# Two-stream feed-forward blocks: gate and up products by seven block products, inner dimension in three chunks

## The chip, the cores and the metric

One NeuronCore of a Trainium2 chip runs the kernel. The metric is the device time of one execution in microseconds (us); shorter is better. The engines are PE (matrix products), DVE (elementwise work on vectors), ACT (casts and activation functions), POOL (idle here) and SP (which issues the DMA loads). Each works through its own queue in order.

## The reference, cut to what matters

Two stacks of two layers are computed one after the other in float32. The first works on one stream of 256 tokens of width 1024. The second works on two streams, `xs` (256 tokens) and `cs` (256 context tokens), with a modulation vector per stream. The block that the change touches is

```python
def ffn_half_step(s, m, i, norm_g, w_in, w_out):
    h = modulate(rmsnorm(s, norm_g), m, i)
    gu = h @ w_in                       # 1024 -> 2 x 2816
    y = (jax.nn.silu(gu[..., :D_FF]) * gu[..., D_FF:]) @ w_out   # 2816 -> 1024
    return s + 0.5 * gate(m, i) * y

def modulation(cond, w_mod, b_mod):
    m = jax.nn.silu(cond) @ w_mod + b_mod    # 1024 -> 9 x 1024
```

Each layer of the second stack runs `ffn_half_step` (step 0) on both streams, a mixer (step 1) with attention over both, and `ffn_half_step` (step 2). In the last layer, step 2 runs on `xs` alone. So three such blocks run on both streams: (layer 0, step 0), (0, 2) and (1, 0).

## The kernel before, in words

Float32 products are made of three matmuls. `parts` splits a tile into a rounded high part (a cast on ACT) and the rest (a subtraction on DVE, the low part); `mm3` adds high x high, high x low and low x high in PSUM. Weights arrive by DMA in tiles `raw` (four in a ring), and `weights` splits them into `whi` and `wlo` (rings of four each). An instruction that needs a slot of a ring waits until the slot's last reader is done. In `mm3` the low part of the weights is read first by the third matmul of a group.

`ffn2` has 22 pairs of 128 gate columns and 128 up columns. A pair is two products of 8 k-tiles on 512 columns (both streams side by side), then silu and product on ACT and DVE, and a split into `g`. After 11 pairs (a half) come eight down steps `d`, each over the 11 `g`s, and `gated_add` puts them onto the stream. The first pairs of a block are computed on the un-normalised stream (`ahead`, `firsts`) while the norm's factor R is being made (`norm_end`), and are corrected afterwards (`rooted`); these are the cover for the norm and for the building of `h` (`streams`).

The modulation vectors are not matmuls: `mod_step` takes one 128x1024 instruction on DVE per column group and stream (tile `junk`; 256 in all), with its weights in `wm` (two slots, one load of 512 KB for two instructions). They are strewn between the other work, in a fixed order; `mod_in(l, step)` and `mod_out` flush what a step still needs. `mix2` is the mixer: latents, convolution and Fourier parts, then heads (`hd`), with output products over the first four tiles (`wa`) between them and the last four at the end (`wo`).

The order of each engine's queue is what a scheduler made of the program at build time; it is fixed when the kernel runs.

Of the kernel before, what the change touches and what calls it, by code (L numbers as in the profile page):

```python
# [25 lines left out]
NU = {(0, 2): 2, (1, 0): 2, (1, 2): 3}  # L26
# [45 lines left out]
def host_arrays(inp):  # L72
# [28 lines left out]
    o["w2u1"], o["w2d1"] = ups(f["ffn1_w_in_2"]), downs(f["ffn1_w_out_2"])  # L101
    o["w2u2"], o["w2d2"] = ups(f["ffn2_w_in_2"]), downs(f["ffn2_w_out_2"])
# [109 lines left out]
class Net:  # L212
# [41 lines left out]
    def r4(self, *shape, more=False):  # L254
        if more:
            x = self.t("r4b", [P, 1028], 4, F32R, pool=self.p_second)
        else:
            x = self.t("r4", [P, 1028], 15, F32R)
# [228 lines left out]
    def mod_out(self, l, step):  # L487
# [3 lines left out]
        for s in range(2):  # L491
# [6 lines left out]
            self.G[s] = G  # L498

# [441 lines left out]
    def ffn1(self, l, R):  # L941
# [4 lines left out]
        first = self.first_two(pre, (0,))  # L946
# [34 lines left out]
        for d in range(KD):  # L981
            if l == 1 and d == 5:

                self.mod_in(0, 0)
                self.h_c = [self.r4(2, 512, more=k >= 4) for k in range(KD)]
            ps = self.ps()[:, :T]
            for half in range(2):
                for k0, k1 in ((0, 6), (6, 11)):
# [3 lines left out]
                    if l == 1 and d in (5, 6):  # L992
                        k = 4 * (d - 5) + 2 * half + (k0 > 0)
                        with self.tc.issue_after(self.split.ins):
                            self.h2(1, self.Rc, self.h_c[k], k)
# [5 lines left out]
            self.add_x(st, d, ps)  # L1001
            if d == 5:
                self.warm(st["sq"])
# [23 lines left out]
    def ahead(self, s, d, n4):  # L1027

        nc = self.nc
        if d == 0 and s == 0:  # L1030
            self.pre2 = []
        if s == 0:

            x = self.r4(1028, more=d >= n4)
            self.pre2.append([[x[:, o:o + n] for o in (b, b + n)] for b, n in ((0, T + 2), (516, T))])
# [37 lines left out]
    def first_two(self, h, order):  # L1073

        W = self.first
        pss = [self.ps() for _ in W]
        for s in order:
            c = slice(s * T, s * T + T)
            for k in range(KD):
                for w, ps in zip(W, pss):  # L1080
                    self.mm3(ps[:, c], (w[0][:, k, :], w[1][:, k, :]), [x[:, c] for x in h[k]], k == 0, k == KD - 1)
        return [ps[:, :len(order) * T] for ps in pss]
# [6 lines left out]
    def ffn2(self, l, step, Rs, nh, ng, n4):  # L1089
        nc, a = self.nc, self.a  # L1090
        ns = len(Rs)
        N = ns * T
        wu, wd = ("w2u1", "w2d1") if step == 0 else ("w2u2", "w2d2")
        third = a[wu][l, 2]
        if l == 0 and step == 0:

            order, xs = (1, 0), self.h_c
            W = self.streams(Rs, (0,), xs, third)
            nu = 1
        else:  # L1100
            order = None
            nu = NU[(l, step)]
            first = self.firsts(ns, [a[wu][l, i] for i in range(2, 2 * nu)])
            third = a[wu][l, 2 * nu]
            xs = [self.r4(2, 512, more=k >= nh) for k in range(KD)]
            W = self.streams(Rs, range(ns), xs, third)
        h = [(x[:, 0, :N], x[:, 1, :N]) for x in xs]
        X = (self.xs, self.cs)
        out = [{} for _ in range(ns)]
        Rs_in, Rs = Rs, []  # L1110
        final = self.next is None
        rate = 2 if l == 0 and step == 0 else 1
        for half in range(2):
            g = []
            for jj in range(HF):
                j = half * HF + jj
                if j >= nu:
                    pss = []
                    for i in range(2):
                        pss.append(self.times(W if 2 * j + i == 2 * nu else a[wu][l, 2 * j + i], h, N))  # L1120
                        self.mod_step(rate)
                elif order:
                    pss = self.first_two(h, order)
                s = self.f2()[:, :N]
                if j >= nu or order:
                    nc.scalar.activation(s, pss[0], AF.Silu)
                    nc.vector.tensor_tensor(s, s, pss[1], ALU.mult)  # L1127
                else:
                    s2 = self.f2()[:, :N]
                    bs = self.rooted((s, s2), first[j], Rs_in)  # L1130
                    for i in range(ns):
# [434 lines left out]
```

## Time and profile before

| | |
|---|---|
| median of 3 runs | 2477.66 us (2476.97 to 2477.69) |
| the profiled execution | 2476.86 us |
| its span, first to last instruction | 2475.1 us |
| PE busy | 2456.9 us, 99% |
| weight loads on PE | 2170.2 us, 88% |
| DVE busy | 1812.9 us, 73% |
| ACT busy | 1197.4 us, 48% |
| mean granted TensorE clock | 0.999 of full speed |

Busy times are shares of one profiled execution; what an engine does while PE is busy costs nothing by itself. Matmuls are pipelined, so the interval between their starts, not their recorded duration, is what one takes.

### The profile page before, as it was taken

What the parts mean: (1) busy time and instruction counts of PE and PEld (TensorE: products, weight loads), DVE (VectorE), ACT (ScalarE), POOL (GpSimd) and SP (SyncE); (2) the same over time, 40 slices, a digit from 0 to 9 for tenths busy, and PEclk for the clock granted to TensorE, in tenths of its full rate; (3) what the DMA queues carried; (4) which work ended last, traced back from release to release, by engine and by line L of the source; (5) the groups of instructions that cost most, each with busy time, mean ns of one, the idle gap of its engine ahead of it and who ended that gap; (6) DMA issues with size and microseconds to landing.
All of it is one profiled execution on the core that took longest, in us unless ns stands there. A gap on an engine that the chain in (4) does not pass through costs nothing.

```text
span 2475.1 us, 39396 instructions
## 1 busy us (share of the span) xinstructions
PE 2456.9 (99%) x15211; PEld 2170.2 (88%) x15211; DVE 1812.9 (73%) x3180; ACT 1197.4 (48%) x2084; POOL 1.2 (0%) x14
## 2 busy tenths in 40 slices
PE   8999999999999999999999999999999999999998
PEld 7999999899999988888887888888888888898998
DVE  8888887988998886776757875655765643688654
ACT  7766665856665522223536632223532223567544
POOL 0000000000000000000000000000000000000000
PEclk9999999999999999999999999999999999999999
DMA  7555657545666664654311344544345742234563
GB/s 251 172 156 181 199 183 235 183 152 172 216 215 205 202 197 149 211 182 125 115 59 42 120 147 127 177 145 125 123 147 163 244 153 74 91 117 139 178 206 120
DMA packets 123851, 395.91 MB, mean 160 GB/s; under 512 B 14352, under 2 KB 17168, under 8 KB 123408
## 3 DMA queue, kind: packets, MB, share of 16 engines
q1 hardware_dynamic: 123664, 393.41, 51.1%
q8 instruction: 119, 1.95, 0.3%
q14 instruction: 68, 0.56, 0.1%
HBM read 392.30 MB, written 1.05 MB: 159 GB/s over the span
## 4 chain that ended last, share of the span: by engine, by line
PE 95%; DVE 2%; ACT 1%; DMA 0%; issue 0%; SPq 0%; DVEq 0%; ACTq 0%
PE wops L305 13%; PE wops L303 13%; PE wops L304 13%; PE dnps L304 6%; PE dnps L305 6%; PE dnps L303 6%; PE upps L305 3%; PE upps L303 3%; PE upps L304 3%; PE qkvps L304 1%; PE qkvps L305 1%; PE qkvps L303 1%; PE cvps L303 1%; PE cvps L305 1%; PE cvps L304 1%; PE latps L304 1%
## 5 line engine op out<-in xcount | busy, mean ns | idle before, releaser
L298 ACT CAST wowhi<-woraw 128x1024 fp32r<-128x1024 f32 (+3 forms) x266 | 246.4, 928 | 581.9 <-PE wops L304 359.6
L305 PE MATMUL wops<-wor,wowlo 128*128 128x512 f32 (+2 forms) x1371 | 480.5, 351 | 0.0
L303 PE MATMUL wops<-wor,wowhi 128*128 128x512 f32 (+2 forms) x1371 | 478.9, 350 | 0.0
L304 PE MATMUL wops<-wor,wowhi 128*128 128x512 f32 (+2 forms) x1371 | 478.6, 349 | 0.0
L299 DVE TENSOR_TENSOR wowlo<-woraw,wowhi 128x1024 fp32r<-128x1024 f32 (+3 forms) x266 | 283.9, 1071 | 216.9 <-ACT wowhi L298 208.7
L304 PEld LDWEIGHTS wops<-wor,wowhi 128*128 128x128 f32 x1371 | 258.0, 188 | 38.0 <-DVE wor L1042 0.2
L305 PEld LDWEIGHTS wops<-wor,wowlo 128*128 128x128 f32 x1371 | 257.9, 188 | 36.5
L303 PEld LDWEIGHTS wops<-wor,wowhi 128*128 128x128 f32 x1371 | 257.5, 188 | 36.5
L298 ACT CAST dnwhi<-dnraw 128x768 fp32r<-128x768 f32 (+2 forms) x144 | 125.1, 871 | 290.7 <-PE dnps L304 184.6
L299 DVE TENSOR_TENSOR dnwlo<-dnraw,dnwhi 128x768 fp32r<-128x768 f32 (+2 forms) x144 | 143.8, 1000 | 69.5 <-ACT dnwhi L298 66.9
L305 PE MATMUL upps<-hr,upwlo 128*128 128x256 f32 x656 | 183.2, 280 | 1.5 <-DVE upwlo L299 1.5
L304 PE MATMUL upps<-hr,upwhi 128*128 128x256 f32 x656 | 183.9, 281 | 0.0
L303 PE MATMUL upps<-hr,upwhi 128*128 128x256 f32 x656 | 183.8, 280 | 0.0
L468 DVE SCALAR_TENSOR_TENSOR dnjunk<-dnwm,cond 128x1024 bf16<-128x1024 f32 x134 | 163.5, 1220 | 2.9 <-DMA dnwm<-in_wm 1.7
L305 PE MATMUL dnps<-dnr,dnwlo 128*128 128x512 f32 (+1 forms) x371 | 142.4, 384 | 0.0
L304 PE MATMUL dnps<-dnr,dnwhi 128*128 128x512 f32 (+1 forms) x371 | 142.2, 383 | 0.0
L303 PE MATMUL dnps<-dnr,dnwhi 128*128 128x512 f32 (+1 forms) x371 | 142.1, 383 | 0.0
L468 DVE SCALAR_TENSOR_TENSOR wojunk<-wowm,cond 128x1024 bf16<-128x1024 f32 x114 | 138.9, 1219 | 0.0
L305 PEld LDWEIGHTS upps<-hr,upwlo 128*128 128x128 f32 x656 | 123.2, 188 | 2.3 <-DVE upwlo L299 2.3
L303 PEld LDWEIGHTS upps<-hr,upwhi 128*128 128x128 f32 x656 | 123.6, 188 | 0.0
L304 PEld LDWEIGHTS upps<-hr,upwhi 128*128 128x128 f32 x656 | 123.1, 188 | 0.0
L1127 DVE TENSOR_TENSOR wof<-wof,wops 128x512 f32<-128x512 f32 (+1 forms) x59 | 35.5, 602 | 110.2 <-PE wops L305 110.2
(690 smaller groups left out, 6197.9 us busy)
## 6 DMA issues: line engine op xcount, KB each, us to landing
woraw<-in_w2u SPq DMA_DIRECT2D x132, 512.0 KB, 3.7
upraw<-in_w1u SPq DMA_DIRECT2D x82, 512.0 KB, 4.3
wowm<-in_wm SPq DMA_DIRECT2D x73, 512.0 KB, 4.4
dnwm<-in_wm SPq DMA_DIRECT2D x67, 512.0 KB, 4.2
dnraw<-in_w2u SPq DMA_DIRECT2D x44, 512.0 KB, 4.2
woraw<-in_w2d SPq DMA_DIRECT2D x48, 384.0 KB, 3.1
woraw<-in_w2d SPq DMA_DIRECT2D x48, 320.0 KB, 2.9
qkvraw<-in_w1q SPq DMA_DIRECT2D x24, 512.0 KB, 4.4
```

The lines of the kernel that those rows point to most:

```text
L298: act = self.nc.scalar.copy(hi, src)
L299: return act, self.nc.vector.tensor_tensor(lo, src, hi, ALU.subtract)
L303: mm(ps, L[0], R[0], start=st, stop=False)
L304: mm(ps, L[0], R[1], start=False, stop=False)
L305: mm(ps, L[1], R[0], start=False, stop=sp)
L468: nc.vector.scalar_tensor_tensor(junk, self.wm, 1.0, self.cond[:, s, :], ALU.mult, ALU.mult, accum_out=self.M[l][s][step][:, j:j + 1])
L1127: nc.vector.tensor_tensor(s, s, pss[1], ALU.mult)
```

## The change

A new `ffn2s` replaces `ffn2` for the three two-stream blocks; `ffn2` remains for the last, single-stream one. Two pairs are made un-normalised as before. The other 20 are a 2x2 block product: rows are the streams, columns gate and up, and the inner 1024 is cut in halves. By Strassen's scheme (Winograd's form) it takes seven block products of 4 k-tiles on 256 columns in place of two products of 8 k-tiles on 512. `sums` builds the seven moving operands (x1, x2, c2, t1 to t4) once per block; `seven` builds, per pair, the seven stationary ones from four 128x512 sums on DVE and four splits: A (11 and 12), B (s2 and s1), C (s3 and 22), D (s4 alone). `begin`, `middle` and `ends` issue the products and what joins them; the last two products of a pair are issued within the next pair. The inner 22 of the down product is cut in chunks of 8, 7 and 7 instead of two halves of 11, so there are 24 down steps a block, each with one weight tile, in place of 16 with two.

The modulation work is spread anew: one `junk` in a pair (all of chunks 1 and 2, the last two of chunk 0), one or two in a down step, and for (0, 2) also in the mixer's projections, its `wa` phase, and a flush `mod_in(l, 2)` in its `wo` phase. Some buffers move: `r4b` has 8 tiles in place of 4, K, Q and the rope table use it, and `es` has two of 1024 in place of three of 512. Block (0, 0) now also makes its first pairs un-normalised.

```diff
-NU = {(0, 2): 2, (1, 0): 2, (1, 2): 3}
+NU = 2
+CHUNKS = ((0, 8), (8, 15), (15, 22))
...
+    def seven(self, gate, up):
+
+        nc = self.nc
+        r1, r2 = self.raw(gate), self.raw(up)
+        h = slice(0, 4), slice(4, 8)
+        s = self.t("es", [P, 1024], 2, pool=self.p_second).rearrange("p (a b) -> p a b", a=8)
+        W = {}
+
+        def split(x, a, b=None):
+            n = x.shape[1]
+            hi, lo = [self.t(t, [P, 1024], 4, F32R)[:, :n * P].rearrange("p (a b) -> p a b", a=n)
+                      for t in ("whi", "wlo")]
+            self.split = self.parts(hi, lo, x)[1]
+            W[a] = hi[:, h[0]], lo[:, h[0]]
+            if b:
+                W[b] = hi[:, h[1]], lo[:, h[1]]
+
+        add = lambda o, a, b: nc.vector.tensor_tensor(o, a, b, ALU.add)
+        split(r1, "11", "12")
+        add(s[:, h[1]], r2[:, h[0]], r2[:, h[1]])
+        add(s[:, h[0]], s[:, h[1]], r1[:, h[0]])
+        split(s, "s2", "s1")
+        add(r2[:, h[0]], r2[:, h[0]], r1[:, h[0]])
+        split(r2, "s3", "22")
+        add(r1[:, h[1]], s[:, h[0]], r1[:, h[1]])
+        split(r1[:, h[1]], "s4")
+        return W
+
+    def product(self, ps, W, B, st, sp):
+        for k in range(4):
+            self.mm3(ps, (W[0][:, k, :], W[1][:, k, :]), self.B7[B][k], st and k == 0, sp and k == 3, True)
...
+                u = self.begin(a[wu][l, 2 * j], a[wu][l, 2 * j + 1])
+                if n or jj >= 6:
+                    self.mod_step(1)
+                if todo:
+                    todo.pop(0)()
+                self.middle(u, todo.pop(0) if todo else lambda: None)
+                x = self.r4(2, 512, more=gmore(jj))
+                g.append((x[:, 0], x[:, 1]))
+                todo = self.ends(u, g[-1])
+            for f in todo:
+                f()
+            if n == 2:
+                self.mod_in(*((l, 1) if step == 0 else (1, 0)))
...
+                self.mod_step(1 if c < 4 else 2, (l, 2, 16))
...
             W = self.weights_half(a["w2o"][l, d, :, 0:4])
+            self.mod_step(1, (l, 2, 16))
```

How the queues change is seen at three places. Names carry the tile's number, and `waits` the engines or DMA queues that must have come so far.

On DVE, one pair of the block (0, 2) before: `wof` is silu(gate) times up, `wor` its low part, `wowlo` low parts of weights, `wojunk` modulation.

```order
L1127 TENSOR_TENSOR wof22887_16241<-wof22887_16241,wops2885_16214 128x512 [waits PE_49,Activation_49]
L299 TENSOR_TENSOR wowlo2910_16359<-woraw2908_16356,wowhi2909_16358 128x1024 [waits DMAHW0_49,Activation_49]
L299 TENSOR_TENSOR wor42888_16244<-wof22887_16241,wor42888_16244 128x512 [waits Activation_49]
L468 SCALAR_TENSOR_TENSOR wojunk2912_16387,M110_139<-wowm2906_16352,cond_471 128x1024
L299 TENSOR_TENSOR wowlo2917_16398<-woraw2915_16395,wowhi2916_16397 128x1024 [waits DMAHW2_49,PE_49,Activation_49]
L468 SCALAR_TENSOR_TENSOR wojunk2920_16428,M100_136<-wowm2919_16426,cond_471 128x1024 [waits DMAHW4_49,DVE_49]
```

A pair had six rows, two of them modulation, and no sum of weights among them.

On DVE, one steady pair in the second chunk of the block (0, 0) now. Low parts: `upwlo2108` is C, `upwlo2110` is D, `upwlo2125` is the next pair's A and `upwlo2127` its B. `upes` and `upraw` with L1161 are sums of weights; L1213, L1218 and L1220 belong to the previous pair's result, `upr4b` is its low part.

```order
L1161 TENSOR_TENSOR upes2123_12696<-upes2123_12696,upraw2121_12692 128x512 [waits DMAHW2_49,DVE_49]
L304 TENSOR_TENSOR upwlo2108_12576<-upraw2101_12561,upwhi2107_12575 128x1024 [waits Activation_49]
L304 TENSOR_TENSOR upwlo2110_12581<-upraw2100_12559,upwhi2109_12580 128x512 [waits PE_49,Activation_49]
L473 SCALAR_TENSOR_TENSOR upjunk2116_12617,M001_131<-upwm2115_12615,cond_471 128x1024 [waits DMAHW7_49]
L1213 SCALAR_TENSOR_TENSOR upf22094_12481<-upps2091_12453,upf22094_12481 128x256
L1161 TENSOR_TENSOR upraw2122_12694<-upraw2122_12694,upraw2121_12692 128x512
L1218 TENSOR_TENSOR upf22094_12481<-upf12096_12511,upsc2097_12530 128x256 [waits PE_49]
L304 TENSOR_TENSOR upwlo2125_12698<-upraw2121_12692,upwhi2124_12697 128x1024 [waits Activation_49]
L1220 SCALAR_TENSOR_TENSOR upf22094_12481<-upf12098_12555,upf22094_12481 128x256 [waits Activation_49]
L1161 TENSOR_TENSOR upraw2121_12692<-upes2123_12696,upraw2121_12692 128x512 [waits DVE_49]
L304 TENSOR_TENSOR upwlo2127_12704<-upes2123_12696,upwhi2126_12703 128x1024 [waits PE_49,Activation_49]
L304 TENSOR_TENSOR upr4b2099_12558<-upf22094_12481,upr4b2099_12558 128x512 [waits Activation_49]
```

The low part of the next A now stands behind D's low part, a junk, a sum of weights and two instructions of the previous pair.

On PE, within the pair whose tiles are 2103 (A), 2105 (B), 2107 (C) and 2109 (D), where the fourth product of the queue ends and the fifth begins:

```order
L308 MATMUL upps2111_12584<-tr41876_11177,upwhi2105_12570 128x256
L309 MATMUL upps2111_12584<-tr41876_11177,upwhi2105_12570 128x256
L310 MATMUL upps2111_12584<-tr41876_11177,upwlo2106_12571 128x256
L308 MATMUL upsc2097_12530<-tr41850_11091,upwhi2089_12449 128x256 [waits DVE_49]
L309 MATMUL upsc2097_12530<-tr41850_11091,upwhi2089_12449 128x256
L310 MATMUL upsc2097_12530<-tr41850_11091,upwlo2090_12450 128x256
```

The fifth product, s4 times c2, is the previous pair's: it reads `upwhi2089`, the previous D, whose slot the present D (`upwhi2109`) takes.

On DVE, the `wo` phase of the layer 0 mixer, before (a gated add is L1086 there, L1042 builds the next block's un-normalised operands, L316 the norm's sum of squares):

```order
L1086 SCALAR_TENSOR_TENSOR xs_75<-wops2745_15435,hdMG2530_14504,xs_75 128x256 [waits PE_49]
L1086 SCALAR_TENSOR_TENSOR cs_8279<-wops2745_15435,hdMG2531_14506,cs_8279 128x256
L299 TENSOR_TENSOR wowlo2772_15568<-woraw2770_15565,wowhi2771_15567 128x512 [waits DMAHW4_49,Activation_49]
L316 TENSOR_TENSOR woS2562739_15417<-woS2562739_15417,wonq2746_15449 128x256 [waits Activation_49]
L1042 SCALAR_TENSOR_TENSOR wor42747_15452<-xs_75,woMA2733_15390,wor42747_15452 128x256 [waits DVE_49,Activation_49]
L316 TENSOR_TENSOR woS2562741_15425<-woS2562741_15425,wonq2748_15458 128x256 [waits Activation_49]
L1042 SCALAR_TENSOR_TENSOR wor42747_15452<-cs_8279,woMA2734_15394,wor42747_15452 128x256 [waits DVE_49,Activation_49]
L1086 SCALAR_TENSOR_TENSOR xs_75<-wops2752_15469,hdMG2530_14504,xs_75 128x256 [waits PE_49]
L1086 SCALAR_TENSOR_TENSOR cs_8279<-wops2752_15469,hdMG2531_14506,cs_8279 128x256
```

And the same phase now, towards its end (a gated add is L1103 here, the norm's sum L321):

```order
L1103 SCALAR_TENSOR_TENSOR cs_8279<-wops2917_16815,hdMG2654_15740,cs_8279 128x256
L473 SCALAR_TENSOR_TENSOR wojunk2879_16678,M002_132<-wowm2878_16676,cond_471 128x1024 [waits DMAHW5_49,DVE_49]
L321 TENSOR_TENSOR woS2562899_16737<-woS2562899_16737,wonq2920_16838 128x256 [waits Activation_49]
L473 SCALAR_TENSOR_TENSOR wojunk2880_16680,M012_135<-wowm2878_16676,cond_471 128x1024 [waits DVE_49]
L1103 SCALAR_TENSOR_TENSOR xs_75<-wops2924_16849,hdMG2653_15738,xs_75 128x256 [waits PE_49]
L473 SCALAR_TENSOR_TENSOR wojunk2882_16684,M002_132<-wowm2881_16682,cond_471 128x1024 [waits DMAHW6_49,DVE_49]
L321 TENSOR_TENSOR woS2562897_16729<-woS2562897_16729,wonq2925_16863 128x256 [waits Activation_49]
L473 SCALAR_TENSOR_TENSOR wojunk2883_16686,M012_135<-wowm2881_16682,cond_471 128x1024 [waits DVE_49]
L304 TENSOR_TENSOR wor4b2926_16866<-woMb2890_16700,wor4b2926_16866 128x2
L1103 SCALAR_TENSOR_TENSOR cs_8279<-wops2924_16849,hdMG2654_15740,cs_8279 128x256
L473 SCALAR_TENSOR_TENSOR wojunk2885_16690,M002_132<-wowm2884_16688,cond_471 128x1024 [waits DMAHW7_49,DVE_49]
```

Between two gated adds now stand four junks or so; the phase has 22 of them, and none before.

## Rows read from the trace of the kernel before

**Rows 1.** The page, first lines: span, then busy time of each engine.

```profile
span 2475.1 us, 39396 instructions
PE 2456.9 (99%) x15211; PEld 2170.2 (88%) x15211; DVE 1812.9 (73%) x3180; ACT 1197.4 (48%) x2084; POOL 1.2 (0%) x14
```

**Rows 2.** PE's waits in the whole span: total us, times, longest.

```profile
PE qkvps L303 <- ACT r L528: 6.3, 1, 6.3
PE upps L305 <- DVE upwlo L299: 1.5, 3, 0.6
...
PE dnps L304 <- DVE dnr4b L1016: 0.2, 1, 0.2
```

**Rows 3.** Windows of 50 us: two-stream FFN, then single-stream FFN.

```profile
core 0: us, PE busy (x) PEld busy (x) DVE busy (x) ACT busy (x) POOL busy (x), PEclk, DMA share, GB/s
1500.00:1550.00 50.00, 50.00 (x217) 40.43 (x216) 28.64 (x46) 11.64 (x16) 0.00 (x0) 1.00 0.43 127
...
2300.00:2350.00 50.00, 50.00 (x425) 50.00 (x424) 30.89 (x43) 23.44 (x38) 0.00 (x0) 1.00 0.58 182
```

**Rows 4.** Timeline of DVE in the l0 step 2 FFN's entry: start, duration, instruction.

```profile
1434.78 0.69 DVE L299 TENSOR_TENSOR wor<-wof,wor 128x512 fp32r<-128x512 f32 x1
1435.39 1.22 DVE L299 TENSOR_TENSOR wowlo<-woraw,wowhi 128x1024 fp32r<-128x1024 f32 x1
1436.52 1.22 DVE L468 SCALAR_TENSOR_TENSOR wojunk<-wowm,cond 128x1024 bf16<-128x1024 f32 x1
1437.66 0.08 DVE L468 DVE_READ_ACCUMULATOR wojunk<-wowm,cond 128x1 f32 x1
```

**Rows 5.** Timeline of PE, then DVE, at the start of that FFN.

```profile
1409.19 0.28 PE L305 MATMUL wops<-hdr4b,wowlo 128*128 128x256 f32 x1
...
1410.72 0.49 DVE L1013 SCALAR_TENSOR_TENSOR wof<-xs,woMA,woR 128x256 f32<-128x256 f32 x1
1411.12 0.48 DVE L1042 SCALAR_TENSOR_TENSOR wor<-cs,woMA,wor 128x256 fp32r<-128x256 f32 x1
...
1413.23 0.42 DVE L340 TENSOR_TENSOR wonq<-wonq,wonq 128x256 f32<-128x256 f32 x1
1413.57 0.48 DVE L1013 SCALAR_TENSOR_TENSOR wof<-xs,woMA,woR 128x256 f32<-128x256 f32 x1
1413.96 0.41 DVE L341 SCALAR_TENSOR_TENSOR woR<-wonq,wonq 128x256 f32<-128x256 f32 x1
1414.30 2.35 DVE L299 TENSOR_TENSOR wowlo<-woraw,wowhi 128x1024 fp32r<-128x1024 f32 x2
```

**Rows 6.** One of ACT's groups by form, 1460 to 1770 us: busy us, mean ns.

```profile
L298 ACT CAST wor<-wof 128x512 fp32r<-128x512 f32 x12 | 7.5, 621 | 0.3 <-DVE wof L1127 0.3
```

**Rows 7.** Timelines: PE to ACT to DVE (1818 us), DVE to PE (651 us).

```profile
1818.39 0.39 PE L304 MATMUL wops<-wor,wowhi 128*128 128x512 f32 x1
...
1818.82 1.05 ACT L298 CAST wowhi<-woraw 128x1024 fp32r<-128x1024 f32 x1 [3.91 <-PE wops L304]
...
1819.90 1.23 DVE L299 TENSOR_TENSOR wowlo<-woraw,wowhi 128x1024 fp32r<-128x1024 f32 x1 [2.58 <-ACT wowhi L298]
...
651.07 1.22 DVE L299 TENSOR_TENSOR upwlo<-upraw,upwhi 128x1024 fp32r<-128x1024 f32 x1
...
652.35 0.39 PE L305 MATMUL upps<-hr,upwlo 128*128 128x256 f32 x1 [0.63 <-DVE upwlo L299]
```

**Rows 8.** Windows of 50 us in the heads' phases, l0 mixer, then l1 mixer.

```profile
1250.00:1300.00 50.00, 50.00 (x250) 41.64 (x249) 26.46 (x42) 17.24 (x29) 0.00 (x0) 1.00 0.15 48
...
1350.00:1400.00 50.00, 49.98 (x277) 38.33 (x276) 37.26 (x90) 30.85 (x80) 0.00 (x0) 1.00 0.32 101
...
2200.00:2250.00 50.00, 48.93 (x321) 42.00 (x320) 38.56 (x82) 35.69 (x80) 0.00 (x0) 1.00 0.20 64
```

**Rows 9.** The page, loads: KB each, median us from issue to landing.

```profile
woraw<-in_w2u SPq DMA_DIRECT2D x132, 512.0 KB, 3.7
...
wowm<-in_wm SPq DMA_DIRECT2D x73, 512.0 KB, 4.4
```

More of the change, by code (lines that the diff above doesn't have):

```diff
@@ L984, in ffn1 @@
                 self.mod_in(0, 0)
-                self.h_c = [self.r4(2, 512, more=k >= 4) for k in range(KD)]
+                for k in range(5):
+                    self.ahead(0, k, 0)
             ps = self.ps()[:, :T]
@@ new lines, in ends, with first, second @@
+    def ends(self, u, out):
+        nc = self.nc
+        W, r1, r3, y = u["W"], u["r1"], u["r3"], u["y"]
+        def first():
+            self.product(r1, W["22"], "t4", False, True)
+            nc.vector.scalar_tensor_tensor(y[:, :T], r1, -1.0, y[:, :T], ALU.mult, ALU.mult)
+        def second():
+            self.product(r3, W["s4"], "c2", False, True)
+            c = y[:, T:]
+            nc.vector.tensor_tensor(c, u["u2"], r3, ALU.add)
+            nc.scalar.activation(c, c, AF.Silu)
+            nc.vector.scalar_tensor_tensor(c, u["u3"], -1.0, c, ALU.mult, ALU.mult)
+            self.parts(out[0], out[1], y)
+        return [first, second]
@@ L1090, in ffn2, with ffn2s @@
+    def ffn2s(self, l, step, Rs, tmore, gmore, n4):
         nc, a = self.nc, self.a
-        ns = len(Rs)
-        N = ns * T
         wu, wd = ("w2u1", "w2d1") if step == 0 else ("w2u2", "w2d2")
[L1094 to L1106, printed above, removed]
@@ L1113, in ffn2 @@
+        return Rs
+    def ffn2(self, l, step, R, nh, ng):
+        nc, a = self.nc, self.a
+        wu, wd = "w2u2", "w2d2"
+        nu = 3
+        self.phase = "e"
+        first = self.firsts(1, [a[wu][l, i] for i in range(2, 2 * nu)])
+        xs = [self.r4(2, 512, more=k >= nh) for k in range(KD)]
+        W = self.streams([R], (0,), xs, a[wu][l, 2 * nu])
+        h = [(x[:, 0, :T], x[:, 1, :T]) for x in xs]
+        out = {}
         for half in range(2):
@@ new lines, in ffn2 @@
+                    Ws.append((k0, k1, self.weights(a[wd][l, d, :, half * HF + k0:half * HF + k1, :])))
+                for k0, k1, W in Ws:
+                    for k in range(k0, k1):
+                        self.mm3(ps, (W[0][:, k - k0, :], W[1][:, k - k0, :]), g[k], k == 0, k == HF - 1)
+                if half == 1 and d:
+                    self.turn(d - 1)
+                self.gated_add(0, d, ps)
+                if half == 1:
+                    self.norm_add(out, d, KD, self.xs[:, d, :])
```

280 lines of the change are left out of this document (187 added, 93 removed).

## The prediction

> **What bounds the kernel now.** I read the page first, then PE's waits, then stretches of 50 us, then single rows of the other engines. The page says that PE is busy 99% of the span, DVE 73% [rows 1]. The list of PE's waits confirms it: seven rows, of which the longest is 6.3 us, once, and the other six come to about 4 us in the whole span [rows 2]. So today whatever takes matmul time away shortens the kernel, as long as DVE and ACT keep up, and whatever makes PE wait lengthens it by the wait. The profiled execution took 2476.86 us, 0.8 under the median of the runs (2477.66); the sum is made against it. About 0.2% (5 us) is what a measurement of this kernel can tell from no change.
>
> **What the change takes from PE.** A stretch of pure 512-column matmuls holds 217 in 50 us, 0.2306 us each; one of 256 columns holds 425, 0.1177 us each [rows 3]. A gate/up pair of a two-stream FFN was 2x8x3 = 48 matmuls of 512 columns, 11.07 us. Seven products of 4 k, 3 matmuls each, are 84 of 256 columns, 9.89 us. That is 1.18 us a pair, and 3 FFNs with 20 such pairs are 60: **-70.8 us**, if PE is never kept waiting. Three chunks in place of two halves leave the down products' matmul count alone.
>
> The Trainium skill (TensorE: Matmul & The Clock Gate, section Back-to-back issue gap) speaks against this: it gives about 81 ns for a sustained matmul of 128 columns and about 131 ns for one of 512. Between these an estimate for 256 is 98 ns, and by it the pair would go from 6.3 to 8.2 us of PE, not down. The trace does not agree: here the ratio of the two widths is 0.51 and 512 columns take 0.2306 us.
>
> **What it puts on DVE, pair by pair.** Before, a pair cost DVE two low parts of 128x1024, a 512 product and a 512 low part; consecutive starts give 1.14 us for 1024 (and for a modulation product, "junk"), 0.61 for 512 [rows 4], so 3.5 us, or 5.8 with two junks, of 11.07. Now there are three low parts of 1024 (3.42), four sums of weights, one low part of D and one of g at 512 (6x0.61), two 256 scalar-tensor-tensor (0.40 each) and three 256 tensor-tensor (0.34 each) [rows 5]: 8.9 us, 10.0 with the junk that stands in nearly every pair of chunks 1 and 2. PE needs 9.89. DVE alone would thus be level with PE. But order decides, and it is in-order.
>
> D (the s4 weights) is the fourth tile of a pair in rings of four, so it takes the slot of the previous pair's D. That slot is read until the previous pair's s4 product, and PE has this as the fifth product of the present pair (the order shown). Counting from the pair's first matmul: five products end at 5x1.41 = 7.06. ACT then casts D: 0.04 to start and 0.62 [rows 6, 7], DVE goes 0.03 later: 7.75. Behind it in DVE's row stand D's low part 0.61, junk 1.14, scalar-tensor-tensor 0.40, a sum 0.61, tensor-tensor 0.34: 10.85; and only then the low part of the next pair's A, 1.22 [rows 4], and 0.06 to PE [rows 7]: 12.13. That operand belongs to the third matmul of the next pair, so the next pair begins at 11.9 (12.13 less 2x0.118), not at 9.89. Without the junk it is 10.75. The cycle closes on itself, since the next D again waits for the fifth product. Per chunk the first transition is free (no earlier s4 in the chunk). Chunk 0 has six Strassen pairs and junks in the last two: 3x0.86 + 2.0 = 4.6; chunks 1 and 2 have seven pairs: 5x2.0 each. 24.6 a FFN, **+74 us**. Bounds: 0 (DVE gets to A's low part before D's slot is free, against the order) and 60x2.0 = 120. I take 74, as every link has a row.
>
> **Ends of the chunks.** The last pair's s4 product ends nine products, 12.7 us, after that pair begins. Behind it stand a 256 tensor-tensor, silu, a scalar-tensor-tensor, ACT's cast and the low part of g: 2.9 us with the handovers, and on DVE's row also the low parts of the first down weights (1.14 each) and one junk, three in chunk 2: near 20 where PE, with 6 or 7 k of down work (3x0.2306 us each) in hand, wants it near 17. I take 2.2, 2.3 and 3.9 for the three chunks, 8.4 a FFN, **+25 us**; bounds 0 and 15 a FFN.
>
> **Entries.** PE's last matmul of the stage before runs until 1409.5, the second stream's R is finished at 1414.3 [rows 5]: 4.9 us. The un-normalised pairs give PE 4x8x3x2 matmuls of 256, 22.6 us, as cover; today this is enough, PE does not wait there [rows 2]. After R the row of DVE now has, up to the fourth tile of x1, 4 of 1024, 10 of 512, 23 scalar-tensor-tensor and 12 tensor-tensor: 23.7 us, and up to the second Strassen pair's A 35.5. PE wants this A at 22.6 + 5x1.41 = 29.7 and gets it at about 40. With the stalls so far counted once, 9 to 10 us each, three entries: **+29 us**; bounds 0 and 35.
>
> **Modulation work moved into the mixer.** The l0 mixer's output phase now has the rest of (0, 2) to do at once. On DVE, from its first gated add to the low part of the next FFN's first weights, stand 22 junks (25.1), 32 scalar-tensor-tensor (12.6), 14 tensor-tensor (4.7), 5 of 512 (3.1), 2 of 1024 (2.3) and some small: 48.7 us. PE's eight output steps are 8x12x0.2306 = 22.1. The weights that follow are late by the difference, **+26 us**; bounds 0 (the junks find room earlier) and 37 if wm's two slots set the pace: 11 loads at (4.4 + 2.3)/2 = 3.35 us [rows 9] are 37 us beside 23 of other work, so 60. Before, no junk stood here. In the heads' phases some 19 (l0) and 16 (l1) junks enter; DVE has 11 to 24 us free in 50 there [rows 8], but its work is links of a chain. 35x1.14 = 40 is the upper end, 0 the lower; about a third, **+12 us**, since the row with least room has PE at 48.93 [rows 8].
>
> The down phases (DVE 4.1 to 4.7 us a step of a low part, one or two junks, two gated adds and in chunk 2 the norm, PE 7 or 8 k x 3 x 0.2306 = 4.8 or 5.5) hide their extra 8 steps' gated adds: if the cover went, 24x0.8 = 19 us. Loads: 1 MB of weights a pair and 0.25 of wm. A raw slot frees one pair ahead, some 6.6 us before it is read, against 3.7 to 4.4 us to land [rows 9]: hidden, and if not 1 to 2 us a pair.
>
> **Sum.** 2476.9 - 70.8 + 74 + 25 + 29 + 26 + 12 = **2572 us**, 3.8% slower.
>
> The Trainium skill (Perfetto Trace Analysis, section Optimization Strategy) says that the same gap repeating on the engine that should be saturated can mean too few buffers for the next tile. By this the 2.0 us would recur in every pair of chunks 1 and 2, which is the cycle above; no run here shows it yet.
>
> **Rivals.**
> A. *Faster: the pair is bound by PE.* If DVE reaches A's low part early, since waits in its row end sooner than I count, pairs come every 9.89 us, the cycle's 74 go, and with them most of the tails and of the junk's cost in the heads: -70.8 + 29 + 26 and a few give about 2465; with entries and output phase hidden too, 2406. For it: DVE's work per pair is just at PE's. Against: the slot. It decides where the work between D's slot and A's low part falls by 2.0 us, about one junk and one sum.
> B. *About the same.* Only the cycle holds and junks hide elsewhere: +74 + 0 to 8 cancel the gain: 2477 to 2485. For: wide lower bounds of the other four terms. Against: all four would have to vanish.
> C. *Slower by less.* The cycle is as above and half of 92 for the rest is hidden: 2500 to 2535.
> D. *Loads come late.* Each pair waits 1 us more for raw weights or wm: +60, 2630. Against it: 1.25 MB in 11.9 us is 105 GB/s, and 182 stand in a stretch today [rows 3].
> E. *256-column matmuls with weights of their own cost more than 0.1177.* At 0.132 the gain is nil, and the time 2640. Rows of 256 with as many weight loads as matmuls (425 and 424) speak against it [rows 3].
>
> **Chances.** The forecast with its bounds (2535 to 2625) 0.5, C 0.17, B 0.06 (half of it within 0.2%), A 0.19, D and E 0.08. The range has to reach down to A's 2465 and up to D: 2463 to 2628 leaves out A's lower part and the far end. The likeliest alone has 2535 to 2610. Slower by over 0.2% 0.77, within 0.2% 0.04, faster 0.19.
>
> **What would show it.** In the profile of the changed kernel: about 352 matmuls (84 in 11.9 us) in 50 us of the up stretches of chunks 1 and 2, against 425 for a PE at its peak; in PE's waits a row "<- DVE upwlo" of 2 us, some ten times a FFN, at the third matmul of a pair; waits of 5 to 10 us behind the sums at the three entries; one wait or several, of some 26 us together, at the end of the l0 mixer. DVE near 85 to 100% in the pairs. If the up stretches show 425 and DVE idles, the cycle is wrong and A holds; if PE waits there for ACT after a DMA, it is D; if PE waits for nothing and yet shows under 425, it is E. My weakest terms are the last two: they rest on counted work beside counted cover, not on a row that shows the wait.

## The result and the profile after

| | before | after |
|---|---|---|
| median, same chip | 2477.47 us (4 runs, 2476.97 to 2477.69) | 2495.11 us (4 runs, 2492.55 to 2496.45) |
| ratio | 1 | 1.007 [1.0053, 1.0088] |
| span of the profiled execution | 2475.1 us | 2494.7 us |
| mean granted TensorE clock | 0.999 | 0.985 |

The changed kernel is slower by 0.7%, 17.6 us. The forecast was 2572 us, with 2535 to 2610 called likeliest: the sign came out, the size was wrong by 77 us. The page's first lines, which answer to [rows 1]:

```profile
span 2494.7 us, 44881 instructions
PE 2413.4 (97%) x17383; PEld 2240.9 (90%) x17383; DVE 2165.6 (87%) x3926; ACT 1396.6 (56%) x2494; POOL 1.2 (0%) x14
```

PE is busy 43.5 us less, some of that at a lower clock; DVE is busy 353 us more. PE's waits over the whole span (total, times, longest), the answer to [rows 2]:

```profile
PE upps L308 <- DVE upf L1089: 16.3, 4, 8.4
PE hdtp L1657 <- ACT hdes L1648: 8.9, 5, 4.5
PE wops L310 <- DVE wowlo L304: 8.7, 1, 8.7
PE wops L308 <- DVE cs L1103: 8.5, 2, 5.6
PE upps L310 <- DVE upwlo L304: 6.7, 5, 3.6
PE qkvps L308 <- ACT r L543: 6.0, 1, 6.0
PE hdsc L308 <- ACT hdr4b L303: 4.7, 3, 2.4
PE wotp L330 <- DVE woS L321: 3.5, 1, 3.5
```

Only the `qkvps` row is wholly old. A repeating wait of 2 us at the pairs is not there: `upwlo` is waited for 5 times, not thirty, and three of these (1.5 us) are old ones in the first stack. The new waits lie in few places: the three entries (7.7, 8.9 and 5.9 us, the `upps` rows and some short ones not shown), the l0 mixer's end (`wops`, `wotp`: 20.7) and the heads (`hdtp`, `hdsc` and three short rows not shown: about 17). Windows of the changed kernel, in the form of [rows 3] and [rows 8]:

```profile
core 0: us, PE busy (x) PEld busy (x) DVE busy (x) ACT busy (x) POOL busy (x), PEclk, DMA share, GB/s
850.00:900.00 50.00, 42.36 (x333) 41.37 (x332) 47.12 (x86) 30.65 (x54) 0.00 (x0) 0.90 0.19 66
1100.00:1150.00 50.00, 50.00 (x419) 49.51 (x418) 48.94 (x83) 31.03 (x58) 0.00 (x0) 1.00 0.43 145
1400.00:1450.00 50.00, 32.25 (x202) 29.84 (x203) 46.47 (x105) 22.75 (x47) 0.00 (x0) 0.76 0.43 146
1450.00:1500.00 50.00, 41.13 (x325) 40.76 (x324) 48.43 (x95) 33.38 (x61) 0.00 (x0) 0.90 0.19 64
1800.00:1850.00 50.00, 44.09 (x355) 43.48 (x355) 48.80 (x95) 34.58 (x63) 0.00 (x0) 0.97 0.18 64
2200.00:2250.00 50.00, 40.46 (x213) 32.85 (x214) 38.37 (x74) 24.42 (x50) 0.00 (x0) 0.86 0.56 182
```

The second line is a steady up stretch: 419 matmuls of 256 columns in 50 us, PE busy throughout, DVE at 48.94 of 50. The other lines are entries, the mixer's end and the heads: there PE waits 6 to 18 us and its granted clock falls below 1. Where 0.90 stands, the engine had the lower of its two levels (1.2 of 2.4 GHz) for a fifth of the window.

By stages (boundaries are the first product of the next block in the trace): up to the l0 mixer 11.7 us are won, in (0, 2) 9.4 and in (1, 0) 11.0; the l0 mixer takes 232.4 us in place of 203.2 (+29.2), the l1 mixer 146.5 in place of 126.7 (+19.8), and the last block 2.7 more. The sum is +19.6, the difference of the two spans. Where the 2.7 in the last block come from was not traced.

Why the pair does not wait is seen in one steady pair of chunk 2 in (0, 0), starts and durations on PE, ACT and DVE:

```profile
1119.18 1.05 ACT L303 CAST upwhi<-upraw 128x1024 fp32r<-128x1024 f32 x1 [0.98 <-PE upps L309]
...
1120.27 1.82 DVE L304 TENSOR_TENSOR upwlo<-upraw,upwhi 128x1024 fp32r<-128x1024 f32 x2
1120.56 0.63 ACT L303 CAST upwhi<-upraw 128x512 fp32r<-128x512 f32 x1
...
1121.91 0.28 PE L308 MATMUL upsc<-tr,upwhi 128*128 128x256 f32 x1
...
1123.41 1.06 ACT L303 CAST upwhi<-upraw 128x1024 fp32r<-128x1024 f32 x1 [0.93 <-PE upsc L309]
1124.50 1.23 DVE L304 TENSOR_TENSOR upwlo<-upraw,upwhi 128x1024 fp32r<-128x1024 f32 x1
...
1126.15 0.28 PE L308 MATMUL upps<-tr,upwhi 128*128 128x256 f32 x1
1126.39 0.28 PE L310 MATMUL upps<-tr,upwlo 128*128 128x256 f32 x1
```

The cast of 512 elements is D. It runs at 1120.56, *before* the previous pair's s4 product begins at 1121.91; the forecast let it wait until that product was over. The wait for that product is on the next row, 1123.41, and belongs to the next pair's A. So the ring doesn't go round in order, and the sentence beside the queue order ahead of the prediction, that the present D takes the previous D's slot, is wrong. The trace doesn't name the slots, but the starts fit this: C takes the slot of its own pair's A (free after two products), D that of the previous C, and the next A that of the previous D. The next A's low part ends at 1125.73; PE needs it at 1126.39 and waits for nothing. The period is 9.95 us, from 1116.20 to 1126.15.

### The profile page after: what moved, and what is told of

Same layout as the page of the kernel before. It is cut to its first block, busy times and chain, and to the rows that moved or that the text cites. A ratio compares the mean times of both kernels' runs of the same rounds, so it can differ in the third digit from the quotient of the medians.

```text
span 2494.7 us, 44881 instructions
## 1 busy us (share of the span) xinstructions
PE 2413.4 (97%) x17383; PEld 2240.9 (90%) x17383; DVE 2165.6 (87%) x3926; ACT 1396.6 (56%) x2494; POOL 1.2 (0%) x14
## 4 chain that ended last, share of the span: by engine, by line
PE 85%; DVE 10%; DMA 2%; ACT 2%; issue 1%; SPq 0%; DVEq 0%; ACTq 0%
PE upps L308 9%; PE upps L310 9%; PE upps L309 9%; PE dnps L308 6%; PE dnps L309 6%; PE dnps L310 6%; PE upsc L309 2%; PE upsc L308 2%; PE upsc L310 2%; PE eps L310 2%; PE eps L308 2%; PE eps L309 2%; DMA cvwm<-in_wm 1%; PE qkvps L309 1%; PE qkvps L310 1%
## 5 line engine op out<-in xcount | busy, mean ns | idle before, releaser
L303 ACT CAST upwhi<-upraw 128x1024 fp32r<-128x1024 f32 (+1 forms) x262 | 249.6, 953 | 225.2 <-PE upps L309 104.1
L304 DVE TENSOR_TENSOR upwlo<-upraw,upwhi 128x1024 fp32r<-128x1024 f32 (+1 forms) x262 | 283.6, 1098 | 27.7 <-ACT upwhi L303 26.2
L308 PE MATMUL upps<-tr,upwhi 128*128 128x256 f32 x1000 | 284.7, 285 | 17.0 <-DVE upf L1089 16.3
L310 PE MATMUL upps<-tr,upwlo 128*128 128x256 f32 x1000 | 282.4, 283 | 5.2 <-DVE upwlo L304 5.2
L309 PE MATMUL upps<-tr,upwhi 128*128 128x256 f32 x1000 | 282.7, 283 | 0.0
L308 PEld LDWEIGHTS upps<-tr,upwhi 128*128 128x128 f32 x1000 | 190.8, 191 | 21.3 <-ACT tr L303 12.4
L310 PEld LDWEIGHTS upps<-tr,upwlo 128*128 128x128 f32 x1000 | 190.3, 191 | 5.7 <-DVE upwlo L304 5.7
L309 PEld LDWEIGHTS upps<-tr,upwhi 128*128 128x128 f32 x1000 | 190.9, 191 | 0.3
L310 PE MATMUL dnps<-upr,dnwlo 128*128 128x256 f32 (+1 forms) x535 | 169.7, 317 | 0.0
L304 DVE TENSOR_TENSOR dnwlo<-dnraw,dnwhi 128x896 fp32r<-128x896 f32 (+3 forms) x146 | 150.1, 1030 | 22.5 <-ACT dnwhi L303 21.7
L309 PE MATMUL dnps<-upr,dnwhi 128*128 128x256 f32 (+1 forms) x535 | 169.4, 317 | 0.0
L308 PE MATMUL dnps<-upr,dnwhi 128*128 128x256 f32 (+1 forms) x535 | 169.2, 317 | 0.0
L309 PE MATMUL dnps<-upr4b,dnwhi 128*128 128x512 f32 (+1 forms) x366 | 141.2, 386 | 0.0
L308 PE MATMUL dnps<-upr4b,dnwhi 128*128 128x512 f32 (+1 forms) x366 | 140.8, 386 | 0.0
```

What stands on the lines that cost most here:

```text
L303: act = self.nc.scalar.copy(hi, src)
L304: return act, self.nc.vector.tensor_tensor(lo, src, hi, ALU.subtract)
L308: mm(ps, L[0], R[0], start=st, stop=False, skip_group_check=skip)
L309: mm(ps, L[0], R[1], start=False, stop=False, skip_group_check=skip)
L310: mm(ps, L[1], R[0], start=False, stop=sp, skip_group_check=skip)
```

## The experiments

**1. The modulation work out of the mixers.** The 62 modulation instructions that the change left to the mixers (43 in l0, 19 in l1) are skipped with their loads, so the outputs are not the reference's; all else stands.

```diff
+                if self.skip:
+                    self.odd = s == 0
+                    continue
```

> The changed kernel without the 62 modulation instructions (and their loads) that run inside the two mixers; the columns they would fill stay zero. Theory (the modulation put into the mixers is what ate the gain): l0 heads and output phase come back to 180 and 22 us from 190 and 54, the l1 mixer to 114 from 133, so 2495 - 60 = about 2435 us, with no half-clock stretch between 1290 and 1440 us nor at 2215. Rival (the mixers are slower because K, Q and the rope table moved into the shared ring and the es tiles are fewer): 2485 to 2495, the waits stay.

Measured: 2440.44 us, 0.9849 [0.9833, 0.9865]. That is 54.7 us below the changed kernel, and the l0 and l1 mixers take 202.9 and 127.1 us, as they did before the change. PE's only wait from 1190 to 1430 is that of the next entry, and heads and output phase together run at full clock:

```profile
1286.00:1396.00 110.00, 109.98 (x606) 87.64 (x604) 86.64 (x192) 72.37 (x176) 0.00 (x0) 1.00 0.23 77
```

The stretch of the changed kernel up to the last wait of that phase, which lies some way into the next block, has 34 matmuls more and takes 41 us more:

```profile
1286.00:1437.00 151.00, 124.43 (x640) 97.61 (x639) 134.79 (x288) 76.04 (x182) 0.00 (x0) 0.90 0.37 121
```

So the moved modulation, not the block products, is what turns a gain of 37 us into a loss of 18.

**2. The same work into the kernel before.** In block (0, 0) one junk a product in place of two, and none in the down steps of its second half; the 38 left over go to the l0 mixer, at the places where the change has them.

```diff
-        rate = 2 if l == 0 and step == 0 else 1
+        rate = 1
...
+                self.mod_step(1 if c < 4 else 2, (l, 2, 16))
```

> The kernel before, with one modulation instruction a product in block (0, 0) in place of two and none in its second half's down steps, so that 38 of them are left to the l0 mixer (in its projections, between its heads, and 16 in its output phase), at the places where the changed kernel has them; no block products, no chunks. Theory (modulation inside the mixer is what costs, with or without the block products): heads + 9, output phase + 16/21 of 32, so 2477 + about 33 = 2510 us, with half-clock stretches there. Rival (the mixer suffers from what the block products leave behind: buffers, order): within 5 us of 2477.

Measured: 2505.97 us, 1.0114 [1.0099, 1.013], with the same waits as in the changed kernel, and no block product in it:

```profile
PE wops L303 <- DVE cs L1086: 10.8, 2, 5.7
...
PE wops L305 <- DVE wowlo L299: 4.2, 2, 2.5
PE hdsc L303 <- ACT hdes L1470: 2.4, 2, 1.4
```

The l0 mixer grew by 22.7 us and the block behind it, where the late weights' wait lies in part, by 6.0 (380.0 against 374.0). Experiments 1 and 2 show the cause from both sides.

**3. The sums at the entries made light.** `sums` makes two of the seven moving operands and uses them for all seven, so the products are not the reference's; the count of matmuls is unchanged. ACT's casts of the left-out operands go too.

```diff
+            two(f, "x1", "t1")
+            for n in ("x2", "t2", "t3"):
+                self.B7[n].append(self.B7["x1"][-1])
+            for n in ("c2", "t4"):
+                self.B7[n].append(self.B7["t1"][-1])
```

> The changed kernel with the operands c2, t1 to t4 and x2 not computed: the first half's normalised tiles stand in for all seven, so DVE has 5.6 us of sums at a block's entry in place of 20.8; the outputs are not the reference's. Theory (DVE's row of sums behind R makes PE wait at the entries, and the wait drops the clock): the waits of 7.7, 8.9 and 5.9 us and the half-clock stretches behind them (10.2, 10.2, 3.4 us) go, 2495 - 22 - 12 = about 2461 us. Rival (the entries wait for PSUM or weights, not for the sums): within 5 us of 2495.

Measured: 2462.1 us, 0.994 [0.9926, 0.9955], 33.0 below the changed kernel. The `upps <- DVE upf` row is gone and the mixers' rows stay:

```profile
PE wops L310 <- DVE wowlo L304: 8.7, 1, 8.7
PE wops L308 <- DVE cs L1103: 8.5, 2, 5.7
```

The blocks (0, 2) and (1, 0) now take 351.3 and 349.8 us against 374.0 and 370.5 before: 22.7 and 20.7 won, of the 23.6 a block that the matmul count promised. The entries' sums, DVE's and ACT's part together, cost 33 us.

**4. A second junk in each pair.** One more modulation product, its result unused, behind each pair's last split.

```diff
+                    with self.tc.issue_after(self.split.ins):
+                        nc.vector.scalar_tensor_tensor(junk, self.wm, 1.0, self.cond[:, 0, :], ALU.mult, ALU.mult,
+                                                       accum_out=spare)
```

> The changed kernel with every modulation instruction of an up phase done twice (48 more of 1.14 us on DVE, no more loads; the second writes to a spare column). Theory (PE sets the pair at 9.96 us and DVE has some 0.55 us left in it): each such pair grows by 0.6 us, 2495 + 29 = about 2524. Rival 1 (there is more room on DVE than the trace shows): 2495 to 2500. Rival 2 (the cycle of the prediction, D's slot to the next A, is closed in reality): every one of the 48 adds its whole 1.14, 2550.

Measured: 2519.42 us, 1.0172 [1.0155, 1.0189]. In the up stretch DVE is nearly full and PE now misses 3.5 us in 50:

```profile
1110.00:1160.00 50.00, 46.45 (x357) 43.69 (x357) 49.33 (x89) 28.17 (x53) 0.00 (x0) 0.98 0.34 118
```

For 1.14 us more of DVE work in each of 48 pairs, the three blocks grew by 9.6, 7.7 and 8.2 us, some 0.5 a pair. So, by this estimate, the pair in the changed kernel stands 0.6 us (1.14 less 0.5) short of being bound by DVE: nearly level, as predicted, on the good side.

**5. The modulation work placed earlier.** Two kernels. `mod_earlier` puts junks into all pairs of chunk 0 and all down steps of the two-stream blocks, and undoes the first stack's thinning of them, so that fewer stay for the mixers; `mod_fit` does the same in the blocks, but leaves the first stack's down steps nearly as they were, and uses the projections of its second layer instead.

```diff
-                if n or jj >= 6:
-                    self.mod_step(1)
+                self.mod_step(1)
...
-                elif d < 5:
+                else:
```

> The changed kernel with all three blocks by seven products, and modulation moved ahead: 52 instructions in the first stack's down phases in place of 16 and 9 there, one in every Strassen pair, two in each down step of chunks 0 and 1, one in each of chunk 2; 16 remain in the l0 mixer, none in the l1 mixer. Theory: the extra ones hide behind PE (DVE was idle 114 us in the first 833) and the mixers regain some 45 of 64 us: 2440 to 2455 us. Rival (DVE has no room in the pairs and down steps): each of the 46 moved ones costs its 1.14 us again, 2485 to 2500.

> The changed kernel, all three blocks by seven products, with modulation moved ahead as in mod_earlier but with 41 instead of 75 instructions in the first stack (8 of them in the second mixer's projection phase, where DVE is idle 3 of 10 us); 27 remain in the l0 mixer, 5 of them in its output phase, none in the l1 mixer. Theory: the first stack keeps its 833 us (mod_earlier lost 10 there), the l0 mixer costs 9 in the heads and 5 in the output phase: 2440 + 15 = about 2455 us. Rival (what remains in the l0 mixer costs in proportion, 27/43 of 41 us): 2466.

Measured: 2461.64 (0.9937 [0.9922, 0.9952]) and 2459.82 us (0.9929 [0.9914, 0.9943]). Both are over their theory's number. In both the l0 mixer still takes 211 us, 8 over the kernel before; in the first, the first stack pays 10 us besides (841.7 against 831.7 us), on waits such as

```profile
PE dnps L308 <- ACT dnwhi L303: 5.2, 4, 1.6
```

Whether its 20 further junks there (52 in place of 32) or the loads of `wm` ahead of the down weights' make these casts late was not told apart.

**6. Block (0, 0) computed directly.** A function of the old form for (0, 0) alone (two halves, products of 8 k on 512 columns, two junks beside each product), block products for (0, 2) and (1, 0). Four junks remain for the mixers.

```diff
-                    Rs = self.ffn2s(l, 0, Rs, [False] * 14, lambda jj: jj > 0, 8)
+                    Rs = self.ffn2d(l, 0, Rs, 8, 7, 8, 2)
```

> The changed kernel with block (0, 0) as direct 512-column products in two halves of 11 again, two modulation instructions a product in it, and down steps of (0, 2)'s first chunk topped up to two; everything is computed, and 4 modulation instructions remain in the mixers (58 fewer). Theory: loses what the seven products gained in that block (12 us) and regains the mixers (60 us): about 2447 us, faster than before by 1.2%. Rival (buffers): 2495 + 12 = 2507.

Measured: 2457.39 us, 0.9919 [0.9905, 0.9934]: 10 us over the expectation, but the fastest version that computes everything, 0.8% under the kernel before and 1.5% under the changed one. It gives up the 11.7 us that this block had won, and has room in it for the junks whose late place cost 55. Its l0 mixer takes 203.4 us.

**7. That, with part of the entry's sums on POOL.** One of three low parts of 512, one difference and the low part of t3 go to the idle engine, for each k.

```diff
-            nc.vector.tensor_tensor(t3, f[:, T:], c1, ALU.subtract)
+            nc.gpsimd.tensor_tensor(t3, f[:, T:], c1, ALU.subtract)
...
+            low.tensor_tensor(x[:, 1], f, x[:, 0], ALU.subtract)
```

> The kernel of direct_00 with a part of the sums on POOL: the subtraction and low part of t3 and the low part of x2 and t4, 5.1 us of DVE's 20.8 at each of the two entries. Theory (DVE's row is what PE waits for at the entries, 8.9 and 4.6 us with some 8 us at half clock behind each): 2457 - 10 to 16 = 2441 to 2447. Rival (POOL is slow or holds DVE up): 2457 or more.

Measured: 2467.22 us, 0.9959 [0.9944, 0.9974], 10 *over* experiment 6. The entry's wait grew:

```profile
PE upps L308 <- DVE upf L1089: 25.6, 2, 15.0
```

and DVE's own rows show why, beside POOL and without it:

```profile
1441.56 0.93 DVE L1114 SCALAR_TENSOR_TENSOR tf<-xs,woMA,woR 128x256 f32<-128x256 f32 x1 [1.16 <-POOL tr L1120]
1442.17 0.90 POOL L1129 TENSOR_TENSOR tf<-tf,tf 128x256 f32<-128x256 f32 x1
1442.41 1.21 DVE L1163 TENSOR_TENSOR upes<-upraw 128x512 f32<-128x512 f32 x1
...
1449.12 0.68 DVE L1163 TENSOR_TENSOR upraw<-upraw,upraw 128x512 f32<-128x512 f32 x1
```

A sum of weights takes 1.21 us while POOL works and 0.68 once it is done, POOL itself 0.9 for what DVE does in 0.4, and DVE waits for POOL's slots besides.

**8. More junks in the convolution phase.** `mod_fit` with twice the junks in the l0 mixer's projections, where DVE is half idle.

```diff
-                self.mod_step(1 if c < 4 else 2, (l, 2, 16))
+                self.mod_step(2 if c < 4 else 4, (l, 2, 16))
```

> mod_fit with the 27 modulation instructions of the l0 mixer drawn together into its latent and convolution phases (2 and 4 behind each projection), none between the heads or in the output phase. Theory (a modulation instruction costs where it stands in a chain between DVE, ACT and PE, and is free where DVE is idle; DVE is idle 21 of 48 us in the convolution phase): heads and output phase come back by 9 + 7 us less a little, 2460 - 10 = about 2450 us. Rival (the two slots of wm, a load of 4.4 us behind every second instruction, hold them up into the heads all the same): 2456 to 2462.

Measured: 2467.16 us, 0.9954 [0.9938, 0.9971], worse by 7. The phase and the heads behind it:

```profile
1239.00:1288.00 49.00, 49.00 (x245) 40.81 (x244) 27.46 (x42) 15.36 (x26) 0.00 (x0) 1.00 0.18 60
1288.00:1394.00 106.00, 94.10 (x482) 71.11 (x481) 88.97 (x192) 56.54 (x139) 0.00 (x0) 0.90 0.28 92
```

DVE still idles 21 us in the first line, and PE misses 12 in the second: the added junks ran in the heads, not in the phase they were written for. By count, of the junks written for the projections seven ran from 1190 to 1288 (six in `mod_fit`) and twenty-one from 1288 to 1394 (nine in `mod_fit`, which has thirteen others there). What held them back is on record: `dft` puts the matrix of the Fourier part into both slots of `wm`, and the next load goes out when its last products have read it, on PE, SP and DVE:

```profile
L310 PE MATMUL cvps<-cvwm,cvr x16: 276/281/292, 1276.6 to 1281.9; 128*128 128x256 f32 x16
...
1282.10 6.41 SPq L471 DMA_DIRECT2D cvwm<-in_wm  x3
...
1285.66 1.23 DVE L473 SCALAR_TENSOR_TENSOR cvjunk<-cvwm,cond 128x1024 bf16<-128x1024 f32 x1 [2.12 <-DMA cvwm<-in_wm]
```

So the slots are the reason, as the rival has it, but because they were lent out from 1229 to 1282, not by the pace of the loads. A third slot was not tried.

**9. The entry's products by k.** The first Strassen pair's two first products take each k as soon as its sums are there, in place of waiting for all. To free their PSUM banks, the first un-normalised pair is corrected ahead of the sums. Once on experiment 6, once on experiment 8.

```diff
+        def each(k):
+            for r, w, b in (("r1", "11", "x1"), ("r2", "12", "x2")):
+                self.mm3(u0[r], (u0["W"][w][0][:, k, :], u0["W"][w][1][:, k, :]), self.B7[b][k], k == 0,
+                         k == 3 and r == "r2", True)
```

> The kernel of direct_00 with the entries in another order: the first un-normalised pair is corrected ahead of the sums, which frees its PSUM banks, and the first Strassen pair's two opening products run k by k as the sums deliver x1 and x2. Theory (at an entry PE waits 8.4 and 4.1 us for a bank that the correction frees behind the whole row of sums): PE does up to 2.1 us of products inside the wait, and the half-clock stretch shrinks: 2457 - 3 to 8 = about 2452 us. Rival (the end of DVE's row decides, whatever PE does before it): 2457.

> mod_cv with the entries of direct_00_kmajor in all three blocks. Theory: the two gains add, 2450 - 7 = about 2443 us, 1.4% under the kernel before. Rival (the entries do not gain): as mod_cv.

Measured: 2468.1 (0.9964 [0.9951, 0.9977]) and 2477.99 us (1.0004 [0.9995, 1.0013]), each 11 over its base. In the entry of (0, 2) one wait of 8.4 us became ten, 8.3 in all (6.6 for ACT's casts of the sums, 1.7 for their low parts), and the hundred microseconds around the entry read, in experiment 6:

```profile
1400.00:1500.00 100.00, 91.18 (x728) 89.61 (x726) 95.59 (x184) 67.20 (x122) 0.00 (x0) 0.97 0.26 91
```

and by k:

```profile
1400.00:1500.00 100.00, 91.45 (x680) 86.99 (x680) 91.00 (x175) 67.17 (x119) 0.00 (x0) 0.91 0.22 78
```

PE is busy as long, but with 48 matmuls fewer: the granted clock is 0.91 against 0.97. DVE's rows of the sums' last low part, first in experiment 6, then by k, show what the edit did besides:

```profile
1440.62 0.68 DVE L304 TENSOR_TENSOR tr<-tf,tr 128x512 fp32r<-128x512 f32 x1
...
1448.94 0.68 DVE L304 TENSOR_TENSOR tr<-tf,tr 128x512 fp32r<-128x512 f32 x1
```

With the correction and its low part ahead of them in DVE's row, the sums begin 7.0 us later (their first low part runs at 1430.53 in place of 1423.53) and end 8.3 us later; the block takes 5.7 us more (362.2 against 356.5). The sums are what the entry waits for, and the edit delayed them. What the order on PE alone would give was not tried.

**10. A slot of its own for D.** The rings of `whi` and `wlo` cut to three, the fourth slot for D alone.

```diff
+        n = self.turns[tag] = self.turns.get(tag, -1) + 1
+        if own or (self.own is False and n % 4 == 3):
+            return self.t("d" + tag, [P, 1024], 1, F32R)
+        return self.t(tag, [P, 1024], 3, F32R)
```

> The changed kernel with the ring of four weight tiles cut into a ring of three and one slot alone: in the Strassen pairs D has that slot to itself, as the prediction assumed, so that it waits for the previous pair's s4 product; A, B and C rotate among the three; other weights take the four in turn. The scheduler then puts the low part of the next A ahead of D's on DVE. Theory (the pair is bound by PE as long as DVE's queue follows the slots; the prediction's error was to join a queue made for one set of slots to another set): 2490 to 2505 us, 420 matmuls in 50 us of an up stretch. Rival (the prediction's cycle): pairs of 11 to 12 us, 2540 or more.

Measured: 2508.26 us, 1.0132 [1.0115, 1.0148]. Now D does wait for the previous pair's s4, as the forecast had it, and still the pair is bound by PE (340 matmuls in 40 us):

```profile
1110.00:1150.00 40.00, 40.00 (x340) 40.00 (x340) 37.98 (x61) 24.66 (x44) 0.00 (x0) 1.00 0.41 131
```

for the scheduler turned the queue round; on DVE and ACT:

```profile
1126.75 1.22 DVE L311 TENSOR_TENSOR upwlo<-upraw,upwhi 128x1024 fp32r<-128x1024 f32 x1
...
1128.42 0.62 ACT L310 CAST updwhi<-upraw 128x512 fp32r<-128x512 f32 x1 [0.97 <-PE upsc L316]
...
1129.10 0.69 DVE L311 TENSOR_TENSOR updwlo<-upraw,updwhi 128x512 fp32r<-128x512 f32 x1
```

The next A's low part (1126.75) now stands ahead of D's (1129.10). The 13 us lost (9 in the profiled execution) lie elsewhere: 6.9 of the 9 in block (0, 0), the two other blocks take as long as in the changed kernel to within 0.7. They were not traced to one place; waits of the down products there for ACT's casts of weights (3.0 us) are among PE's waits.

## Why the prediction was right or wrong

**The gain held.** -70.8 us by matmul count. Without the entries' sums the blocks win 22.7 and 20.7 of 23.6 (experiment 3), and 256-column matmuls came at 419 in 50 us, near the 425 that were counted on. Rival E, which needs 0.132 us each, is out; so is D, since no wait for a load of weights shows in the up stretches.

**The cycle, +74, was wrong: 0.** The failed step is "D ... takes the slot of the previous pair's D". It came from counting allocations in a ring of four. The rows at 1119 to 1126 show D's cast before the s4 product and the next A's cast after it. The order of DVE's queue was known and showed it: D's low part stood *ahead* of the next A's, which a scheduler that expects D's slot late would not do; given that slot (experiment 10), it put them the other way round. I joined the queue of one assignment of slots to the waits of another. That combination was in no kernel, and what it would cost was not tried. For the pair rival A is what happened: the wait in DVE's row ended sooner than counted, though it named no slot. Its total of 2465 did not come, as it let most of the junks' cost in the heads go.

The Trainium skill (Perfetto Trace Analysis, section Optimization Strategy) says that a repeating gap can mean too few buffers. No gap repeats in the pairs here (PE busy 50.00 of 50 at 1100), so the rule has nothing to say of them; its use for a cycle not yet seen was mine.

**Ends of the chunks, +25: 0.** No wait of the first down products is among PE's waits. The step that failed is DVE's row behind the last s4 product. At the end of chunk 1 in (0, 0) that product is over on PE at 1040.95 and the last low part of g on DVE at 1045.11, 4.2 us later and not some 7: the low parts of the first two down weights had started at 1035.56 and 1040.47, ahead of the tail. PE had the first k of the down steps to do meanwhile, some of them already between the pair's last products. The down phases and the pairs' loads were hidden, as priced.

**Entries, +29: 33.** Right in place and cause, DVE's row of sums behind R (experiment 3). What PE waits for is another thing: the forecast let it do five products of the first Strassen pair and stand at the second pair's A. At the entry of (0, 2) it stands at the first product of the first pair, until DVE has read an un-normalised product from PSUM (L1089, the correction), which comes 24.2 us after R:

```profile
1463.05 0.42 DVE L1089 TENSOR_TENSOR upf<-fps,woR 128x256 f32<-128x256 f32 x1
...
1463.62 0.55 PE L308 MATMUL upps<-tr,upwhi 128*128 128x256 f32 x1 [8.40 <-DVE upf L1089]
```

That the size agrees is partly luck: the waits themselves are 22.5 us, not 29; the rest fits the lower clock beside them (0.90, 0.90 and 0.97 in the three windows), which the forecast left out.

**Modulation in the mixers, +38 (26 and 12): 55.** Right in place and mechanism, too small (experiments 1 and 2). The waits in the output phase are 20.7 of the 26; I gave the clock nothing. The heads' share was guessed at a third of DVE's added work; their waits are about 17 us, and the l1 mixer alone lost 19.4 (146.5 against 127.1 without its junks). In l0 even the junks written for the projections add to the heads: the `wm` slots are lent to the Fourier part there too (see experiment 8), the next load goes out at 1280.94. A junk that waits for `wm` stands in DVE's row ahead of a link of the heads' chain:

```profile
2225.34 1.23 DVE L473 SCALAR_TENSOR_TENSOR cvjunk<-cvwm,cond 128x1024 bf16<-128x1024 f32 x1 [0.92 <-DMA cvwm<-in_wm]
...
2226.49 0.16 DVE L1645 RECIPROCAL hdsm<-hdsm 128x2 f32<-128x2 f32 x1
...
2226.68 0.72 ACT L1648 ACTIVATE hdes<-hdes,hdsm 128x512 f32<-128x512 f32 x1 [0.94 <-DVE hdsm L1645]
...
2227.46 0.47 PE L1657 MATMUL hdtp<-ident,hdes 128*128 128x128 f32 x1 [4.48 <-ACT hdes L1648]
```

DVE waits for the load, the reciprocal stands behind the junk, ACT waits for the reciprocal and PE for ACT.

**The sum.** -70.8 + 33 + 55 = +17, against 17.6 measured. The error of 77 is 74 + 25 - 4 - 17 = 78, less 1 for the base and rounding: two terms that are not there, a wrong slot and a tail that DVE had cleared in time, and two that were too small. That the sign came out is luck: without the two false terms the same sum gives 2473, a gain of 4 us. Rival B's sum is off as well: 2476.9 - 70.8 + 74 + 0 to 8 is 2480 to 2488, not 2477 to 2485.

## What to carry to other kernels

When an in-order queue comes from a scheduler, read the slots off the queue (who stands ahead of whom, which cast waits for which product), not off the order of allocation; a wait derived from one and an order taken from the other can describe a program that doesn't exist. When a stretch is filled up, its displaced work has to be priced at the place where it lands: here 62 instructions, 71 us of an engine that was 73% busy, cost 55 us, since a free share in a phase of chains is not room, and the best of the remedies tried was to give up the change in the one block whose cover they needed.

## What the runs showed of the hardware

The granted clock falls where PE waits, and stays low for a while after: a wait costs more than its length. Behind the wait of 8.40 us that ends at 1463.62, PE is busy throughout the next window of the changed kernel, yet does 29 matmuls in 5 us, where 419 in 50 are 42:

```profile
1465.00:1470.00 5.00, 5.00 (x29) 5.00 (x28) 4.98 (x14) 2.88 (x7) 0.00 (x0) 0.58 0.01 2
```

Over the changed kernel the mean is 0.985 against 0.999, an estimated 35 us of full speed over the span, some of it while PE was idle anyway.

POOL is not a free helper beside DVE: a 512-element sum on DVE took 1.21 us with POOL at work for part of it and 0.68 without (experiment 7). The Trainium skill (GPSIMD Engine Reference, section 1. Specifications) says that the two share their SBUF interfaces and contend where a DVE instruction has two SBUF inputs; the rows agree.
